# The boundary between two blocks of a decoder trunk: sample tokens join the norms of their token group, and the second group's sums stand ahead of the first group's second norm

## The chip, the core and the metric

The kernel runs on one core of one Trainium2 chip, in one launch. The metric is the device time of an execution in microseconds, the median of several runs. TensorE is PE in the profile (its weight loads PEld), VectorE is DVE, ScalarE is ACT, GpSimd is POOL, and SyncE is SP, whose queue issues most of the DMAs.

## What is computed

The reference is one step of a decoder trunk with two layers. Each layer has a token mixer (a gated DeltaNet in layer 0, an HGRN in layer 1) and then a feed-forward block with a short convolution. 1024 prompt tokens and 64 sample tokens (8 sequences of 8) share all weights; the width is 1024. What matters here is what stands between two blocks:

```python
for layer in range(DEPTH):
    sh1, sc1, g1, sh2, sc2, g2 = jnp.split(mod, N_MOD, axis=-1)
    h = _rmsnorm(x, norm_pre_mix[layer]) * (1 + sc1) + sh1
    out, S, ... = mixer(h, ...)
    x = x + (1 + g1) * _rmsnorm(out, norm_post_mix[layer])      # boundary: norm, gate, residual,
    h = _rmsnorm(x, norm_pre_ffn[layer]) * (1 + sc2) + sh2      # and the next block's norm
    out, fbuf = _conv_ffn(h, ...)
    x = x + (1 + g2) * _rmsnorm(out, norm_post_ffn[layer])
```

`_rmsnorm` divides a token's 1024 values by the root of their mean square. The scales, shifts and gates are one vector for the prompt and one for each sample sequence.

## The kernel before

Activations lie transposed: 1024 channels are 8 tiles of 128 partitions (the index m), and tokens run along the free axis. Tokens are cut into three groups. In the order in which every stage takes them they are called 0, 1 and 2 here, as in the strings below. Group 0 has 256 prompt tokens and the 64 sample tokens behind them (its matmuls are 320 wide), groups 1 and 2 have 384 prompt tokens each. Matmuls run on a high and a low part of every operand, so each step over 128 channels is three matmuls (L113 to L115). A block ends with an output product whose first half is done for all groups and whose second half (tile `pf`) is left to the boundary; the next block begins with products named `pg` (feed-forward) or `pp` (HGRN) on its input h.

`boundary()` (L330 to L400) is called four times: after the DeltaNet mixer, after the first feed-forward block, after the HGRN mixer, and at the end. It runs stages in the order of a string (L35 to L37): ORDM after a mixer, ORDF after the first feed-forward block, ORDL at the end. The stages of a group are:

- S (`st_sum`): per m the last twelve matmuls of the output (`pf`), their sum into `acc` on DVE (L352; L354 for the sample tokens), the squares on ACT (L236), their column sums on PE (`pn`, L228), a copy by ACT (`sqp`, L242) and a small product that leaves one sum per token and partition (`pc`, L245).
- R (`st_res`): 1/sqrt on DVE in some twelve tiny instructions (L251, L85 to L91), its spread over 128 partitions by PE (L218), and per m the gate (L364, DVE), the residual (L366, on POOL or DVE by the tables POOLM, POOLF and POOLL) and a DMA of the new residual to HBM.
- P (`st_pre`): the next block's norm, which squares the residual that R left (L236), sums it (L228, L242, L245), takes 1/sqrt, spreads it (L218), and makes h in three steps per m: L264 on DVE, L265 on ACT, L266 on DVE.
- s (`st_smp`): residual and next norm of the 64 sample tokens alone: squares (L280), a reduction of 1.0 us on DVE (L282), a product (L283), a 1/sqrt chain of their own (tiles `nwss`, `nwts`, `snr`), the spread (L275), and the elementwise steps (L380 to L382, L299 to L305), twice the whole way.

The program order of the stages is the order of priority of a scheduler that writes one fixed queue for each engine; an engine takes its queue in order. Buffers bound how far PE can run ahead: `pf`, `pg` and `pp` share a ring of three PSUM banks, and squares and `sqp` share a ring of two SBUF tiles, each of which holds two squares. A `pf` of tile m needs the bank that DVE's L352 of tile m-3 left.

Of the kernel before, what the change touches and what calls it, by code (L numbers as in the profile page):

```python
# [13 lines left out]
AF = mybir.ActivationFunctionType  # L14
ALU = mybir.AluOpType
# [3 lines left out]
D = 1024  # L19
# [23 lines left out]
def trunk_kernel(ctx: ExitStack, tc: tile.TileContext, a: dict, o: dict):  # L43
# [7 lines left out]
    def big(tag, shape=(128, NTOK), dt=F32, name=None, bufs=None):  # L51
        return main.tile(list(shape), dt, tag=tag, name=name or tag, bufs=bufs or {"xp": 2, "wraw": 3, "whl": 3}.get(tag, 1))
# [4 lines left out]
    def ps(tag, name=None):  # L57
        return psp.tile([128, 512], F32, tag=tag, name=name or tag, bufs={"mm": 3, "mx": 3, "rc": 2}[tag])
# [146 lines left out]
    def mod(l, i):  # L205
        return mods[l][:, 8 * i:8 * i + 8, :]
# [11 lines left out]
            mm(rb[:, 128 * j:128 * j + 128], r[:, j:j + 1].to_broadcast([128, 128]), ident, start=True, stop=True)  # L218
        return rb

    def row_sums(src, n):


        pn = ps("rc", name="pn")

        def add(m, s):
            q = m % 4
            return mm(pn[32 * q:32 * q + 32, :n], ones[:, :32], s, start=(m < 4), stop=(m >= 4), tile_position=(0, 32 * q))  # L228

# [12 lines left out]
        nc.scalar.activation(pb[:, :n], pn[:, :n], AF.Copy)  # L242
        pc = ps("mx", name="pc")
        for j in range(n // 128):
            mm(pc[:, 384 + j:385 + j], pb[:, 128 * j:128 * j + 128], selq, start=True, stop=True)  # L245
        return pc

    def row_rsqrt(pc, nt):

        v = small("pnv", [128, 3], bufs=2)  # L250
        nc.vector.tensor_scalar(v[:, :nt], pc[:, 384:384 + nt], 1.0 / D, EPS, op0=ALU.mult, op1=ALU.add)  # L251
        r = small("pnr", [128, 3], bufs=2)
        rsqrt(r[:, :nt], v[:, :nt], nt, "a")
        return bcast_rows(pc, r, nt)

    def prenorm(l, xg, n, isc, ish, hgt):

        rb = row_rsqrt(row_sums(xg, n), n // 128)
        sc, sh = mod(l, isc), mod(l, ish)
        pt = big("D10", [128, 2, 512], name="pnt")  # L260
        for m in range(8):
            t = pt[:, m % 2, :n]
            h = hgt[:, 0, m, :n]
            nc.vector.scalar_tensor_tensor(t, xg(m), sc[:, m, 0:1], rb[:, :n], op0=ALU.mult, op1=ALU.mult)  # L264
            nc.scalar.activation(h, t, AF.Identity, bias=sh[:, m, 0:1])  # L265
            nc.vector.scalar_tensor_tensor(hgt[:, 1, m, :n], t, sh[:, m, 0:1], h.bitcast(F32), op0=ALU.add, op1=ALU.subtract)  # L266
# [69 lines left out]
    def boundary(step, l, ig, kind, acc, acc_s, fin, nxt, hname):  # L336


        hgs = [None] * 3
        gw = mod(l, ig)  # L340
        pcs = [None] * 3

        def part(g):
            t0, n = GRP[g][0], GP[g]
            return t0, n, lambda m: acc[m][:, t0:t0 + n]

        def st_sum(g):
            t0, n, am = part(g)

            def total(m):  # L350
                p = fin(g, m)
                nc.vector.tensor_tensor(am(m), am(m), p[:, :n], op=ALU.add)  # L352
                if g == 2:
                    nc.vector.tensor_tensor(acc_s[:, m, :], acc_s[:, m, :], p[:, 256:320], op=ALU.add)  # L354
                return am(m)

            pcs[g] = row_sums(total, n)

        def st_res(g):
            t0, n, am = part(g)  # L360
            xg = load_x(step, g)
            rb = row_rsqrt(pcs[g], n // 128)
            for m in range(8):
                nc.vector.scalar_tensor_tensor(am(m), am(m), gw[:, m, 0:1], rb[:, :n], op0=ALU.mult, op1=ALU.mult)  # L364
                eng = nc.gpsimd if m in (POOLM if kind == 1 else POOLF if nxt is not None else POOLL)[GORD.index(g)] else nc.vector
                eng.tensor_tensor(am(m), am(m), xg(m), op=ALU.add)  # L366
                nc.sync.dma_start(out=xd[step + 1][m, :, t0:t0 + n], in_=am(m))

        def st_pre(g):
            t0, n, am = part(g)  # L370
            if nxt is not None:
                hgs[g] = new_hg(g, hname + str(g))
                prenorm(nxt[0], am, n, nxt[1], nxt[2], hgs[g])

        def st_smp():
            x_s = load_xs(step)
            pc = ps("mx", name="pcs")
            t = ssum(acc_s, pc, 0)
            rb = srow(pc, 0)
            nc.vector.tensor_tensor(v4(t), v4(acc_s), seqb(gw), op=ALU.mult)  # L380
            nc.vector.tensor_tensor(t, t, rb, op=ALU.mult)
            nc.vector.tensor_tensor(x_s, x_s, t, op=ALU.add)  # L382
            nc.gpsimd.dma_start(out=xsd[step + 1], in_=x_s)
            if nxt is not None:
                prenorm_s(nxt[0], nxt[1], nxt[2], hgs[2], x_s, pc)

        for w in (ORDM if kind == 1 else ORDF if nxt is not None else ORDL).split():
            if w == "s":
                st_smp()
            else:  # L390
                dict(S=st_sum, R=st_res, P=st_pre)[w[0]](GORD[int(w[1])])
# [1124 lines left out]
```

## Time and profile before

| what | value |
|---|---|
| median of three runs | 3280.22 us (3267.7 to 3284.62) |
| the profiled execution | 3271.93 us, its span 3270.2 us |
| PE busy | 3156.9 us, 97% |
| DVE, ACT, POOL busy | 1667.2, 1099.0, 275.9 us |
| the boundaries in the span | about 811 to 915, 1688 to 1790, 2371 to 2475 and 3205 to 3270 us |

PE is busy nearly all the time, so the profile is read for the stretches in which it is not. Rows of the timeline give the start of a group of equal instructions, its duration, engine, line, what it writes and reads, how many there are, and in brackets how long the engine was idle just ahead of it and what ended that. A table of windows gives each engine's busy time in a stretch and the granted TensorE clock (PEclk, 1.00 is 2.4 GHz and .50 is 1.2 GHz).

### The profile page before, as it was taken

Reading aid. Unit: us, or ns where it says so; the run is one execution under the profiler, and the core shown is the slowest. Engines: PE = TensorE matmul, PEld = TensorE weight load, DVE = VectorE, ACT = ScalarE, POOL = GpSimd, SP = SyncE. Lnnn points to the kernel's source line nnn. Section 1 sums busy time; section 2 is a strip of 40 time slices with the busy share of each in tenths; the row PEclk is TensorE's granted clock in tenths of the full one; section 3 lists DMA queues with packets and bytes.
Section 4 is the critical chain, followed back from the end, with each engine's and each line's share of the span. In section 5 each row is a group of like instructions: output and inputs, shape, how many; then the busy total and the mean of one; then the engine's idle time right before and its main releaser. Section 6 shows DMA issues by size and latency. Waiting matters only on the chain.

```text
span 3270.2 us, 61821 instructions
## 1 busy us (share of the span) xinstructions
PE 3156.9 (97%) x25457; PEld 2940.0 (90%) x25457; DVE 1667.2 (51%) x3819; ACT 1099.0 (34%) x2619; POOL 275.9 (8%) x623
## 2 busy tenths in 40 slices
PE   7999999999899999999998999999998999999997
PEld 5888888889799999999996999999888999999997
DVE  6776777773742333333357555554465233334345
ACT  5444444443433312222234333332343332222222
POOL 0111111110100000000000000000010000000002
PEclk9999999999999999999998999999999999999999
DMA  6333333234322222222322111122621111111113
GB/s 208 96 106 102 99 105 97 80 115 157 97 76 86 84 85 84 81 86 81 95 71 92 64 61 58 59 86 66 199 91 50 46 46 43 46 46 46 41 62 106
DMA packets 164642, 277.94 MB, mean 85 GB/s; under 512 B 20064, under 2 KB 91488, under 8 KB 164360
## 3 DMA queue, kind: packets, MB, share of 16 engines
q1 hardware_dynamic: 145976, 236.28, 22.3%
q0 software_dynamic: 14976, 37.08, 3.8%
q8 instruction: 200, 3.28, 0.4%
q10 hardware_dynamic: 3408, 0.63, 0.1%
q14 instruction: 82, 0.67, 0.1%
HBM read 222.44 MB, written 51.43 MB: 84 GB/s over the span
## 4 chain that ended last, share of the span: by engine, by line
PE 88%; DVE 5%; ACT 2%; DMA 2%; issue 2%; POOL 1%; ACTq 0%; SPq 0%; DVEq 0%; POOLq 0%
PE pp L114 7%; PE pp L113 7%; PE pp L115 6%; PE pu L113 5%; PE pg L113 5%; PE pg L114 5%; PE pg L115 5%; PE pu L115 5%; PE pu L114 5%; PE pd L113 5%; PE pd L115 5%; PE pd L114 5%; PE pf L113 1%; PE pf L114 1%; PE pf L115 1%
## 5 line engine op out<-in xcount | busy, mean ns | idle before, releaser
L113 PE MATMUL pp<-h,wi 128*128 128x384 f32 (+1 forms) x1536 | 516.2, 338 | 3.3 <-ACT h L304 2.5
L114 PE MATMUL pp<-h,wi 128*128 128x384 f32 (+1 forms) x1536 | 516.9, 337 | 0.7 <-DVE h L305 0.6
L115 PE MATMUL pp<-h,wi 128*128 128x384 f32 (+1 forms) x1536 | 514.6, 336 | 1.7 <-issue 1.7
L113 PE MATMUL pg<-h,wg 128*128 128x384 f32 (+1 forms) x1056 | 346.6, 329 | 0.0
L114 PE MATMUL pg<-h,wg 128*128 128x384 f32 (+1 forms) x1056 | 345.5, 328 | 0.8 <-DVE h L305 0.8
L113 PE MATMUL pu<-h,wu 128*128 128x384 f32 (+1 forms) x1056 | 346.3, 328 | 0.0
L115 PE MATMUL pg<-h,wg 128*128 128x384 f32 (+1 forms) x1056 | 346.0, 328 | 0.0
L115 PE MATMUL pu<-h,wu 128*128 128x384 f32 (+1 forms) x1056 | 344.8, 327 | 0.0
L114 PE MATMUL pu<-h,wu 128*128 128x384 f32 (+1 forms) x1056 | 344.3, 326 | 0.0
L113 PEld LDWEIGHTS pp<-h,wi 128*128 128x128 f32 x1536 | 291.5, 190 | 19.6 <-issue 11.3
L113 PE MATMUL pd<-mh,wd 128*128 128x384 f32 (+1 forms) x912 | 299.6, 330 | 0.0
L114 PEld LDWEIGHTS pp<-h,wi 128*128 128x128 f32 x1536 | 291.5, 190 | 7.0 <-DVE wi L107 1.2
L115 PE MATMUL pd<-mh,wd 128*128 128x384 f32 (+1 forms) x912 | 297.4, 326 | 0.0
L114 PE MATMUL pd<-ml,wd 128*128 128x384 f32 (+1 forms) x912 | 297.1, 326 | 0.0
L115 PEld LDWEIGHTS pp<-h,wi 128*128 128x128 f32 x1536 | 291.4, 190 | 5.6 <-issue 3.5
L113 PEld LDWEIGHTS pu<-h,wu 128*128 128x128 f32 x1056 | 198.2, 188 | 7.8 <-issue 6.2
L113 PEld LDWEIGHTS pg<-h,wg 128*128 128x128 f32 x1056 | 199.0, 189 | 6.2 <-issue 4.9
L114 PEld LDWEIGHTS pg<-h,wg 128*128 128x128 f32 x1056 | 199.0, 188 | 2.5 <-issue 1.2
L598 DVE TENSOR_TENSOR facc<-facc,pd 128x384 f32<-128x384 f32 (+1 forms) x192 | 97.5, 510 | 203.2 <-PE pd L115 203.2
L115 PEld LDWEIGHTS pg<-h,wg 128*128 128x128 f32 x1056 | 199.1, 189 | 0.0
L115 PEld LDWEIGHTS pu<-h,wu 128*128 128x128 f32 x1056 | 198.2, 188 | 0.0
L114 PEld LDWEIGHTS pu<-h,wu 128*128 128x128 f32 x1056 | 198.2, 188 | 0.0
(450 smaller groups left out, 5708.6 us busy)
## 6 DMA issues: line engine op xcount, KB each, us to landing
adaw<-in_ada_w SPq DMA_DIRECT2D x96, 512.0 KB, 3.9
wgr<-in_w_gu SPq DMA_DIRECT2D x88, 256.0 KB, 2.8
wur<-in_w_gu SPq DMA_DIRECT2D x88, 256.0 KB, 2.6
wir<-in_w_gin SPq DMA_DIRECT2D x64, 256.0 KB, 2.7
wdr<-in_w_dn SPq DMA_DIRECT2D x64, 256.0 KB, 2.5
wir<-in_w_hin SPq DMA_DIRECT2D x64, 256.0 KB, 2.7
og<-ohl SPq DMA_DIRECT2D x32, 384.0 KB, 8.2
xg<-xd SPq DMA_DIRECT2D x24, 384.0 KB, 4.7
```

The lines of the kernel that those rows point to most:

```text
L113: mm(out, wh, rh(k), start=(first and i == 0), stop=False)
L114: mm(out, wh, rl(k), start=False, stop=False)
L115: mm(out, wl, rh(k), start=False, stop=(last and i == len(ks) - 1))
L598: nc.vector.tensor_tensor(am, am, p[:, :n], op=ALU.add)
```

## The change

The stage s is gone. The squares of the sample tokens stand beside those of group 0, so that the `pn` matmuls of that group are 320 wide, one more `pc` matmul takes their sums, and a third column of the small tiles carries them through the group's 1/sqrt chain. One more spread (128x64) gives their factor. Their gate and residual are part of R of group 0, their norm is part of P of group 0. The orders are new, too: the sums S1 stand ahead of P0, and after a mixer S2 stands ahead of P1, as it did after the feed-forward block before.

```diff
-ORDM = "S0 R0 P0 S1 s R1 P1 S2 R2 P2"
-ORDF = "S0 R0 P0 S1 s R1 S2 P1 R2 P2"
-ORDL = "S0 S1 R0 s R1 S2 R2 P0 P1 P2"
+ORDM = "S0 R0 S1 P0 R1 S2 P1 R2 P2"
+ORDF = "S0 R0 S1 P0 R1 S2 P1 R2 P2"
+ORDL = "S0 S1 R0 R1 S2 R2"
...
-    def row_sums(src, n):
+    def row_sums(src, n, smp=None):
...
+        n0, n = n, n + (0 if smp is None else NS)
...
-                nc.scalar.activation(s, src(m), AF.Square)
+                nc.scalar.activation(s[:, :n0], src(m), AF.Square)
+                if smp is not None:
+                    nc.scalar.activation(s[:, n0:], smp[:, m, :], AF.Square)
...
+        if smp is not None:
+            mm(pc[:64, 386:387], pb[:, n0:n], selq, start=True, stop=True)
...
-        rsqrt(r[:, :nt], v[:, :nt], nt, "a")
+        if smp:
+            nc.vector.memset(v[64:, 2:3], 1.0)
+            nc.vector.tensor_scalar(v[:64, 2:3], pc[:64, 386:387], 1.0 / D, EPS, op0=ALU.mult, op1=ALU.add)
+            rsqrt(r, v, 3, "a")
+            mm(pc[:, 256:320], r[:64, 2:3].to_broadcast([64, 128]), ident[:64, :64], start=True, stop=True)
+        else:
+            rsqrt(r[:, :nt], v[:, :nt], nt, "a")
...
-    def prenorm(l, xg, n, isc, ish, hgt):
+    def prenorm(l, xg, n, isc, ish, hgt, x_s=None):
...
+        if x_s is not None:
+            norm_apply_s(l, isc, ish, hgt, x_s, small("S2", [128, 8, NS], name="sqs"), srow_b(rb), slice(0, 8))
...
+            if g == 2:
+                t = small("S2", [128, 8, NS], name="sqs")
+                nc.vector.tensor_tensor(v4(t), v4(acc_s), seqb(gw), op=ALU.mult)
+                nc.vector.tensor_tensor(t, t, srow_b(rb), op=ALU.mult)
+                nc.vector.tensor_tensor(smp[0], smp[0], t, op=ALU.add)
+                nc.gpsimd.dma_start(out=xsd[step + 1], in_=smp[0])
...
-        def st_smp():
...
-                prenorm_s(nxt[0], nxt[1], nxt[2], hgs[2], x_s, pc)
```

(In the code g is 2 for the group that the strings call 0.) The line numbers of the changed kernel differ: its L365 is L352 here, L379 is L364, L277 to L279 are L264 to L266, L237 and L239 are L236, L229 is L228, L245 is L242, L248 and L250 are L245, and L313 to L317 are L301 to L305.

The queues show where the work went. DVE's queue in the first boundary, around the last four sums of group 2 into `acc` (tiles acc_9356 to acc_9503 are m = 4 to 7). Before:

```order
L89 TENSOR_TENSOR nwts<-snr 64x1
L364 SCALAR_TENSOR_TENSOR acc_9454<-acc_9454,mod_91,pc 128x384
L90 TENSOR_TENSOR nwts<-nwts,nwxs 64x1
L364 SCALAR_TENSOR_TENSOR acc_9503<-acc_9503,mod_91,pc 128x384
L91 SCALAR_TENSOR_TENSOR snr<-nwts,snr 64x1
L352 TENSOR_TENSOR acc_9356<-acc_9356,pf 128x384
L89 TENSOR_TENSOR nwts<-snr 64x1
L352 TENSOR_TENSOR acc_9405<-acc_9405,pf 128x384
L90 TENSOR_TENSOR nwts<-nwts,nwxs 64x1
L352 TENSOR_TENSOR acc_9454<-acc_9454,pf 128x384
```

The same place after the change:

```order
L277 SCALAR_TENSOR_TENSOR pnt<-acc_9503,mod_91,pc 128x256
L379 SCALAR_TENSOR_TENSOR acc_9258<-acc_9258,mod_91,pc 128x384
L279 SCALAR_TENSOR_TENSOR h_9943<-pnt,mod_91,h_9943 128x256 x2
L379 SCALAR_TENSOR_TENSOR acc_9307<-acc_9307,mod_91,pc 128x384
L379 SCALAR_TENSOR_TENSOR acc_9356<-acc_9356,mod_91,pc 128x384
L379 SCALAR_TENSOR_TENSOR acc_9405<-acc_9405,mod_91,pc 128x384
L379 SCALAR_TENSOR_TENSOR acc_9454<-acc_9454,mod_91,pc 128x384
L379 SCALAR_TENSOR_TENSOR acc_9503<-acc_9503,mod_91,pc 128x384
L365 TENSOR_TENSOR acc_9356<-acc_9356,pf 128x384
L365 TENSOR_TENSOR acc_9405<-acc_9405,pf 128x384
L365 TENSOR_TENSOR acc_9454<-acc_9454,pf 128x384
L365 TENSOR_TENSOR acc_9503<-acc_9503,pf 128x384
```

The sixteen instructions of group 0's norm, and three of the sample tokens with them, now stand right ahead of these sums, in between those of R1; before, they stood among the sums of S1, and what stood between those of R1 was the sample tokens' 1/sqrt.

ACT's queue in the same boundary, with tile numbers. Before, where pn_10110 are the sums of P1 and sq_10184 the squares of S2:

```order
L236 ACTIVATE sq_10124<-acc6_9454 128x384
L236 ACTIVATE sq_10124<-acc7_9503 128x384
L242 ACTIVATE sqp_10131<-pn_10110 128x384
L236 ACTIVATE sq_10184<-acc0_9160 128x384
L236 ACTIVATE sq_10184<-acc1_9209 128x384
L236 ACTIVATE sq_10215<-acc2_9258 128x384
L236 ACTIVATE sq_10215<-acc3_9307 128x384
L304 ACTIVATE h12_9785<-sqs_10027 128x8x64
```

After, where pn_10086 are the sums of S2 and sq_10227 the squares of P1:

```order
L237 ACTIVATE sq_10118<-acc3_9307 128x384
L278 ACTIVATE h12_9943<-pnt_10008,mod0_91 128x256
L316 ACTIVATE h12_9943<-sqs_10002 128x8x64
L278 ACTIVATE h12_9943<-pnt_10008,mod0_91 128x256 x7
L237 ACTIVATE sq_10153<-acc4_9356 128x384
L237 ACTIVATE sq_10153<-acc5_9405 128x384
L237 ACTIVATE sq_10184<-acc6_9454 128x384
L237 ACTIVATE sq_10184<-acc7_9503 128x384
L245 ACTIVATE sqp_10219<-pn_10086 128x384
L237 ACTIVATE sq_10227<-acc0_9160 128x384
L237 ACTIVATE sq_10227<-acc1_9209 128x384
```

P1's eight squares moved from ahead of S2's to behind the last of them and its copy.

PE's queue in the same boundary, around the spread for P1 (L218). Before, three matmuls of it stand among the products `pg`, ahead of the last sums of S2:

```order
L113 MATMUL pg<-h_9785,wg 128x320
L114 MATMUL pg<-h_9785,wg 128x320
L115 MATMUL pg<-h_9785,wg 128x320
L113 MATMUL pg<-h_9785,wg 128x320
L218 MATMUL pc<-c_ident,pnr 128x128 x3
L228 MATMUL pn<-sq,ones 32x384 x4
L114 MATMUL pg<-h_9785,wg 128x320
```

After, the spreads for P1 and R2 are one row of six, right behind all of P1's sums:

```order
L113 MATMUL pg<-h_9943,wg 128x320
L114 MATMUL pg<-h_9943,wg 128x320
L115 MATMUL pg<-h_9943,wg 128x320
L229 MATMUL pn<-sq,ones 32x384 x8
L248 MATMUL pc<-c_selq,sqp 128x1 x3
L218 MATMUL pc<-c_ident,pnr 128x128 x6
L113 MATMUL pg<-h_10225,wg 128x384
```

The spread for P1 moved behind S2, and now goes together with that for R2.

## Rows read from the trace of the kernel before

**Rows 1.** The page's first part: busy time, share of the span, instructions.

```profile
PE 3156.9 (97%) x25457; PEld 2940.0 (90%) x25457; DVE 1667.2 (51%) x3819; ACT 1099.0 (34%) x2619; POOL 275.9 (8%) x623
```

**Rows 2.** What PE waited for: us in total, times, longest us.

```profile
PE pn L228 <- ACT sq L236: 28.7, 20, 4.7
...
PE pcs L275 <- DVE snr L91: 5.7, 1, 5.7
```

**Rows 3.** Windows of the first boundary: us; busy time by engine; PEclk, DMA share, GB/s.

```profile
880.00:898.00 18.00, 13.26 (x92) 12.03 (x96) 15.53 (x39) 7.07 (x13) 0.00 (x0) 1.00 0.10 35
898.00:908.30 10.30, 6.88 (x32) 4.62 (x25) 5.70 (x24) 5.10 (x13) 2.08 (x9) 0.50 0.27 96
```

**Rows 4.** Timeline of DVE in the first boundary: P0's norm, R1, last sums of S2.

```profile
846.44 0.55 DVE L352 TENSOR_TENSOR acc<-acc,pf 128x384 f32<-128x384 f32 x1
846.91 0.88 DVE L266 SCALAR_TENSOR_TENSOR h<-pnt,mod,h 128x256 fp32r<-128x256 f32 x2
847.70 0.87 DVE L264 SCALAR_TENSOR_TENSOR pnt<-acc,mod,pc 128x256 f32<-128x256 f32 x2
...
860.53 0.68 DVE L382 TENSOR_TENSOR x_s<-x_s,sqs 128x512 f32<-128x512 f32 x1
...
863.44 0.60 DVE L364 SCALAR_TENSOR_TENSOR acc<-acc,mod,pc 128x384 f32<-128x384 f32 x1
...
865.34 0.60 DVE L364 SCALAR_TENSOR_TENSOR acc<-acc,mod,pc 128x384 f32<-128x384 f32 x1
865.86 0.78 DVE L89 TENSOR_TENSOR nwts<-snr 64x1 f32<-64x1 f32 x1
...
871.38 0.54 DVE L352 TENSOR_TENSOR acc<-acc,pf 128x384 f32<-128x384 f32 x1
```

**Rows 5.** Timeline of PE in the first boundary: R1's spread, P1's, P2's sums.

```profile
862.23 0.83 PE L218 MATMUL pc<-c_ident,pnr 128*128 128x128 f32 x6
...
871.97 0.44 PE L113 MATMUL pf<-og,wo 128*128 128x384 f32 x1 [1.40 <-DVE acc L352]
...
879.83 0.93 PE L218 MATMUL pc<-c_ident,pnr 128*128 128x128 f32 x6
...
897.67 1.23 PE L228 MATMUL pn<-sq,ones 128*32 128x384 f32 x8 [4.74 <-ACT sq L236]
...
903.83 1.44 PE L245 MATMUL pc<-c_selq,sqp 128*128 128x1 f32 x6 [0.67 <-ACT sqp L242]
```

**Rows 6.** A window of the matmuls of `pf` (128x384) alone, in the first boundary.

```profile
829.10:832.20 3.10, 3.10 (x19) 3.10 (x19) 0.98 (x2) 1.00 0.00 0
```

**Rows 7.** Timeline of ACT in the first boundary: the last of P1's squares.

```profile
872.43 0.52 ACT L236 ACTIVATE sq<-acc 128x384 f32<-128x384 f32 x1 [0.44 <-POOL acc L366]
```

**Rows 8.** Timeline of PE in the second boundary, after the feed-forward block.

```profile
1733.51 0.83 PE L218 MATMUL pc<-c_ident,pnr 128*128 128x128 f32 x6
...
1747.11 0.63 PE L113 MATMUL pp<-h,wi 128*128 128x320 f32 x1 [2.51 <-ACT h L304]
1747.94 1.50 PE L228 MATMUL pn<-sq,ones 128*32 128x384 f32 x8 [0.20 <-ACT sq L236]
...
1763.24 2.93 PE L218 MATMUL pc<-c_ident,pnr 128*128 128x128 f32 x12 [2.44 <-DVE pnr L91]
...
1785.19 0.83 PE L245 MATMUL pc<-c_selq,sqp 128*128 128x1 f32 x6 [0.33 <-ACT sqp L242]
```

**Rows 9.** Timeline of DVE in the second boundary.

```profile
1746.31 1.01 DVE L352 TENSOR_TENSOR facc<-facc,pf 128x384 f32<-128x384 f32 x2
...
1766.74 1.90 DVE L266 SCALAR_TENSOR_TENSOR h<-pnt,mod,h 128x384 fp32r<-128x384 f32 x2
...
1770.14 1.14 DVE L266 SCALAR_TENSOR_TENSOR h<-pnt,mod,h 128x384 fp32r<-128x384 f32 x2
```

**Rows 10.** Timeline of ACT in the second boundary, between squares of P1 and `sqp`.

```profile
1757.81 1.28 ACT L1201 ACT_TABLE_LOAD   x1
```

**Rows 11.** Timeline of PE at the end: the last spread.

```profile
3258.54 1.65 PE L218 MATMUL pc<-c_ident,pnr 128*128 128x128 f32 x6 [2.42 <-DVE pnr L91]
```

More of the change, by code (lines that the diff above doesn't have):

```diff
@@ L245, in row_sums, with row_rsqrt @@
             mm(pc[:, 384 + j:385 + j], pb[:, 128 * j:128 * j + 128], selq, start=True, stop=True)
+        if smp is not None:
+            mm(pc[:64, 386:387], pb[:, n0:n], selq, start=True, stop=True)
         return pc
-    def row_rsqrt(pc, nt):
+    def row_rsqrt(pc, nt, smp=False):
         v = small("pnv", [128, 3], bufs=2)
@@ L252, in row_rsqrt @@
         r = small("pnr", [128, 3], bufs=2)
-        rsqrt(r[:, :nt], v[:, :nt], nt, "a")
+        if smp:
[5 more added lines that the diff above has]
+            rsqrt(r[:, :nt], v[:, :nt], nt, "a")
         return bcast_rows(pc, r, nt)
-    def prenorm(l, xg, n, isc, ish, hgt):
-        rb = row_rsqrt(row_sums(xg, n), n // 128)
+    def prenorm(l, xg, n, isc, ish, hgt, x_s=None):
+        rb = row_rsqrt(row_sums(xg, n, x_s), n // 128, x_s is not None)
         sc, sh = mod(l, isc), mod(l, ish)
+        if x_s is not None:
+            norm_apply_s(l, isc, ish, hgt, x_s, small("S2", [128, 8, NS], name="sqs"), srow_b(rb), slice(0, 8))
         pt = big("D10", [128, 2, 512], name="pnt")
@@ L291, in v4, with srow_b @@
         return t.rearrange("p m (s t) -> p m s t", t=8)
-    def prenorm_s(l, isc, ish, hgt, x_s, pc):
-        t = ssum(x_s, pc, 256)
-        norm_apply_s(l, isc, ish, hgt, x_s, t, srow(pc, 256), slice(0, 8))
+    def srow_b(pc):
+        return pc[:, 256:256 + NS].unsqueeze(1).to_broadcast([128, 8, NS])
     def norm_apply_s(l, isc, ish, hgt, x_s, t, rb, ms):
@@ L341, in boundary @@
         pcs = [None] * 3
+        smp = []
         def part(g):
@@ L355, in total @@
                 return am(m)
-            pcs[g] = row_sums(total, n)
+            pcs[g] = row_sums(total, n, acc_s if g == 2 else None)
         def st_res(g):
@@ L361, in st_res @@
             xg = load_x(step, g)
-            rb = row_rsqrt(pcs[g], n // 128)
+            if g == 2:
+                smp.append(load_xs(step))
+            rb = row_rsqrt(pcs[g], n // 128, g == 2)
             for m in range(8):
@@ L367, in st_res @@
                 nc.sync.dma_start(out=xd[step + 1][m, :, t0:t0 + n], in_=am(m))
+            if g == 2:
+                t = small("S2", [128, 8, NS], name="sqs")
[3 more added lines that the diff above has]
+                nc.gpsimd.dma_start(out=xsd[step + 1], in_=smp[0])
         def st_pre(g):
@@ L372, in st_pre @@
                 hgs[g] = new_hg(g, hname + str(g))
-                prenorm(nxt[0], am, n, nxt[1], nxt[2], hgs[g])
-        def st_smp():
[L376 to L384, printed above, removed]
-                prenorm_s(nxt[0], nxt[1], nxt[2], hgs[2], x_s, pc)
+                prenorm(nxt[0], am, n, nxt[1], nxt[2], hgs[g], smp[0] if g == 2 else None)
         for w in (ORDM if kind == 1 else ORDF if nxt is not None else ORDL).split():
[L388 to L391, printed above, removed]
+            dict(S=st_sum, R=st_res, P=st_pre)[w[0]](GORD[int(w[1])])
         return hgs
```

## The prediction

> **What bounds the kernel now.** The page's first part comes first: PE is busy 97% of the span [rows 1], so the time is PE's work plus the stretches in which PE stands still or runs at the lower clock. The change leaves nearly all matmuls alone, so only these stretches can move. What PE waited for tells where they are: the dearest single cause is the column sums waiting for ACT's squares, 28.7 us in twenty waits, which is the work of the boundaries; the sample tokens' own 1/sqrt costs 5.7 us once [rows 2]. The windows of the first boundary show both kinds of loss: from 880 to 898 us PE is busy 13.26 of 18.00 us, and from 898.0 to 908.3 it is busy 6.88 of 10.30 us at a granted clock of .50 (1.2 GHz), after having been half idle just before [rows 3]. So I follow PE, DVE and ACT through one boundary, from R1's spread to P2's sums. P2's sums are my mark: behind them ACT frees the banks of the waiting products in both queues, and what is left of PE's work is the same. The shift of that mark is what a boundary costs or gains. A boundary after a mixer occurs twice (about 811 and 2371 us, the same queues), the one after the feed-forward block once, the end once.
>
> **The change part by part.** *Sample tokens.* Taken away per boundary are two reductions, two chains of 1/sqrt on 64 rows, two squares of 512 columns and two spreads; added are eight squares of 64 columns, twice, one column in an existing chain, one `pc` and one spread. DVE saves most of it, but little of it stands where PE waits, except in the second boundary: there PE waits 5.71 us for that 1/sqrt [rows 2] and then 2.51 us for the sample tokens' h [rows 8]. Both named waits must go. What is late there next is counted below.
>
> *P0 behind S1.* This is the edit that I think decides. Before, P0's norm lies under the sums of S1: two L264 and two L266 take 0.79 and 0.78 us, and one sum L352 of 0.47 us goes with them, from 846.44 to 848.48 [rows 4]; PE has S1's matmuls meanwhile, so it costs nothing. After, DVE's queue has these sixteen instructions between R1's spread and the last four sums of S2. This cover is gone, and what waits behind them is S2: tile m = 7 of `pf` needs the bank of m = 4, which the first of these sums frees. Before, that sum starts at 871.38 and the matmul that waited for it at 871.97 [rows 4, 5].
>
> *Term 1, from R1's spread to that sum.* Before: 862.23 [rows 5] to 871.38, 9.15 us. After: 1.2 us from spread to first use (862.23 to 863.44 [rows 4, 5]), four pairs of P0 at 1.57 us (the two figures above), 6.3 us, three instructions of the sample tokens at 0.60 to 0.68 us (the size of L382 [rows 4]), 2.0 us, and R1's eight L364 at 0.52 us (865.34 to 865.86 [rows 4]), 4.2 us: 13.7 us. P0's L266 now also lie beside POOL's residual adds. Beside such an add two L266 took 1.90 us, without one 1.14 [rows 9], so 0.76 us; I take one such pair, 14.5 us. That is 5.4 us more. The spread itself comes earlier, since L381 and L382 and the sample tokens' tiny instructions leave the chain ahead of it: two at 0.60 us and some 0.2 us, 1.4 us. Term 1: +4.0 us; ends +1.5 (the spread 3 us earlier, no add met) and +6 (two more pairs meet an add).
>
> That a VectorE instruction is held up by an add on GpSimd is also what the Trainium skill says, in "SBUF — State Buffer", section "Who interferes with whom": with two SBUF inputs it contends with a GpSimd instruction that reads SBUF, and whichever starts second is blocked for the whole of the other. The row shows part of an add, not a whole one. By the rule all four pairs could be held, and term 1 would end some 2 us higher; that speaks against the change, which puts P0 where R1's adds are.
>
> *Term 2, from that sum to P1's spread.* Before: 871.38 to 879.83 [rows 4, 5], 8.45 us, because P1's squares ran as R1's residuals came, the last at 872.43 [rows 7], ahead of S2's. After, they stand behind all of S2's squares and their copy. First come twelve matmuls of m = 7 (19 of them in 3.10 us [rows 6], so 2.0 us), a sum of 0.54 us [rows 4] and a square of 0.52 us [rows 7]: 3.1 us. For the rest the second boundary is the pattern, since there S2 stood ahead of P1 already and the two spreads were one row: from the last sums of S2 at 1747.94 to that row at 1763.24, 15.3 us [rows 8]. Of these 1.28 us are a table load between P1's squares and their copy [rows 10], which the first boundary has not: 14.0 us. Together 17.1 us, 8.6 us more; as part of the pattern ran at 1.2 GHz, which I don't expect to the same extent, I take 7.5. Ends +5.5 and +10.5.
>
> *Term 3, from P1's spread to P2's sums.* Before: 879.83 to 903.83 [rows 5], 24.0 us, with R2's scaling behind P1's norm and a wait of 4.74 us in P2's sums. After, P1's norm and R2's scaling share DVE from one row of spreads on, as in the second boundary: 1763.24 to 1785.19 [rows 8], 21.95 us. Term 3: -2 us; ends -4 and 0.
>
> First boundary: 4.0 + 7.5 - 2 = +9.5 us; twice, +19. If all ends fell one way it would be 3 or 16.5; I take 5 to 13 us each.
>
> *Second boundary.* S2 was ahead of P1 before, so terms 2 and 3 are 0. P0's norm, which lay under S1's matmuls here too, joins R1's stretch, which already held the sample tokens. Two of the last sums ran at 1746.31 [rows 9]. After: from R1's spread at 1733.51 [rows 8], the same 13.7 us and five residual adds that DVE keeps by POOLF (0.47 us each, the size of L352), 16.0 us, less 1 us for an earlier spread: 1748.5. With one pair beside an add, 1749.3. So +3 us; the wait for the sample tokens' h (1747.11) is hidden behind it. One more us if a bank is late as above: +4, ends +1 and +7. The 5.71 and 2.51 us don't come back as gain, because what stands in their place is as late.
>
> *The end.* No P there; S0, S1, R0, R1, S2, R2 stay as they were, without the sample stage, and the last spread at 3258.54 [rows 11] hangs on S2. 0 us, ends -2 and +1.5.
>
> Sum: 19 + 4 + 0 = +23 us; from the ends so taken +9 (10 + 1 - 2) to +34 (26 + 7 + 1.5). On the profiled execution, 3271.93 us, that is 3295; this execution is 8.3 us under the median, 3280.22, on which it is 3303. The new time is a median too, so I go nearer to that: 3301 us.
>
> **The rivals.** *Even.* DVE gets rid of some 7 us of sample work per boundary (two reductions of 1.0 us, two chains, squares on ACT), and if the queue's head start is worth that, the late norm is paid for: term 1 falls to its lower end, term 2 to 4 us because PE stays at full speed, and a boundary after a mixer costs 3 us, the second one gains 4 to 6. For: the waits in rows 2. Against: the saved work is not on the stretch from R1's spread on, save for the tiny instructions between the L364. Time: 3280 +- 8 us.
>
> *Faster.* PE stays fed: group 0's h is complete before S2's last tile needs a bank, so that PE takes `pg` products under S2's late sums, and all named waits go: 5.71 + 2.51 in the second boundary, 4.74 + 0.67 in each after a mixer, and half of 10.30 us at half clock in each. That is 8.2 + 10.8, and up to 5 more: some 20 us less, 3260 us. It decides if DVE is through P0 before PE has run `pf` to m = 7. Against: PE's queue has m = 7 ahead of the `pg` products, and an engine takes its queue in order.
>
> *Worse than forecast.* The idle stretch of PE, ahead of the late sum, is followed by a stretch at 1.2 GHz, as at 898.0 [rows 3], and the pairs of P0 all meet POOL's adds: the upper ends, +33 us, 3313 us.
>
> *The change doesn't do what it says.* P0 in front of S2's sums would be harmless if the queue had the sums first; the queues show otherwise, so this has no chance of its own.
>
> **How the numbers follow.** Forecast 0.50, even 0.28, faster 0.14, worse 0.08. 0.5% is about what a measurement can tell from no change, 16 us here: 3264 to 3297. The forecast's own range is 3291 to 3311; about two thirds of it lie over 3297. Slower: 0.34 + 0.08, and 0.02 of the even case: 0.44. Same: 0.16 + 0.26: 0.42. Faster: 0.14. The range leaves out the faster case and half of the worse one: 3270 to 3314.
>
> **What would show it.** In DVE's timeline, the first of S2's last four sums about 14 us behind R1's spread, and PE idle for some 8 us just ahead of it; a stretch at .50 there. P1's spread at about 891 us and as a row of twelve. P2's sums some 9 us later against the first `pf` of the boundary. The second boundary without waits on `snr`, but with one of similar size on `acc` sums or P0's h. If PE's idle time ahead of S2's last tile is under 3 us, term 1 is wrong; if P1's spread follows the late sum by under 12 us, term 2 is; if the second boundary got shorter by over 5 us, the named waits were what bound it.

## The result, and the profile after

| | before | after |
|---|---|---|
| median of six runs each | 3276.03 us (3267.7 to 3284.62) | 3300.05 us (3297.24 to 3306.24) |
| ratio after to before | | 1.0077, interval 1.0064 to 1.009 |
| the profiled execution, its span | 3271.93, 3270.2 us | 3299.28, 3297.5 us |

The change makes the kernel 24 us slower, 0.77%; 3301 us was forecast. In the page's first part PE has the same 25457 matmuls, as in [rows 1], and 11.6 us more busy time (the mean granted clock of the two traces is 0.986 before and 0.980 after); DVE has 84 instructions and 19.5 us less:

```profile
PE 3168.5 (96%) x25457; PEld 2946.6 (89%) x25457; DVE 1647.7 (50%) x3735; ACT 1102.7 (33%) x2668; POOL 278.3 (8%) x623
```

So work was saved, and time was lost. Where, PE's waits in the whole span say (us in total, times, longest us). The wait for the sample tokens' 1/sqrt of [rows 2] is gone; what PE waits for instead are sums into the accumulators, 9.2 us at a time after a mixer and 11.6 us after the feed-forward block:

```profile
PE pn L229 <- ACT sq L237: 21.0, 13, 2.5
PE pf L113 <- DVE acc L365: 18.4, 2, 9.2
PE pp L113 <- DVE facc L365: 11.6, 1, 11.6
PE pc L218 <- DVE pnr L91: 10.0, 5, 2.4
```

The first boundary in PE's timeline of the changed kernel; these lines answer to [rows 5]. PE runs out of `pf` after R1's spread, and 16 us pass until the tile that needs the late sum:

```profile
855.77 1.38 PE L218 MATMUL pc<-c_ident,pnr 128*128 128x128 f32 x10
...
871.65 0.69 PE L113 MATMUL pf<-og,wo 128*128 128x384 f32 x1 [9.20 <-DVE acc L365]
...
888.85 2.93 PE L218 MATMUL pc<-c_ident,pnr 128*128 128x128 f32 x12 [2.44 <-DVE pnr L91]
...
910.05 1.44 PE L248 MATMUL pc<-c_selq,sqp 128*128 128x1 f32 x6 [0.67 <-ACT sqp L245]
```

DVE's timeline of the same stretch answers to [rows 4]. P0's L279 and R1's L379 stand ahead of S2's last sums L365, and DVE is busy from 856.51, its first use of the spreads, to 872.5. The last line is the sum of m = 7, whose matmuls waited for the first of these sums:

```profile
861.21 1.63 DVE L279 SCALAR_TENSOR_TENSOR h<-pnt,mod,h 128x256 fp32r<-128x256 f32 x2
...
864.07 1.61 DVE L279 SCALAR_TENSOR_TENSOR h<-pnt,mod,h 128x256 fp32r<-128x256 f32 x2
...
866.90 1.60 DVE L279 SCALAR_TENSOR_TENSOR h<-pnt,mod,h 128x256 fp32r<-128x256 f32 x2
...
868.43 2.70 DVE L379 SCALAR_TENSOR_TENSOR acc<-acc,mod,pc 128x384 f32<-128x384 f32 x5
871.05 1.47 DVE L365 TENSOR_TENSOR acc<-acc,pf 128x384 f32<-128x384 f32 x3
875.85 0.55 DVE L365 TENSOR_TENSOR acc<-acc,pf 128x384 f32<-128x384 f32 x1 [3.33 <-PE pf L115]
```

Windows of it (us; busy time of PE, PEld, DVE, ACT, POOL; PEclk, DMA share, GB/s) answer to [rows 3]. From 854.6 to 867.5 PE is busy 7.85 of 12.90 us, and behind that the granted clock is .50 (1.2 GHz) for 7.5 us, in which PE stands still for more than half:

```profile
854.60:867.50 12.90, 7.85 (x46) 6.06 (x45) 11.33 (x26) 4.26 (x9) 2.88 (x4) 0.92 0.23 67
867.50:875.00 7.50, 3.35 (x10) 3.35 (x11) 5.02 (x9) 1.45 (x3) 5.56 (x6) 0.50 0.51 186
```

To compare traces whose stretches ahead of a boundary differ, every boundary is measured from its first `pf` matmul. A second trace of the kernel before was taken among the experiments; its execution (3275.45 us) lies nearer to the median. Lengths to the last `pc` matmul of P2, the mark of the prediction, and from one first `pf` to the next (the last column to the end of the span):

| | 1st | 2nd | 3rd | first pf to next first pf |
|---|---|---|---|---|
| before | 93.7 | 97.8 | 93.7 | 876.8, 683.0, 834.4, 64.8 |
| before, second trace | 95.9 | 98.2 | 96.2 | 879.5, 684.3, 837.0, 64.9 |
| after | 106.7 | 106.0 | 107.0 | 890.8, 689.2, 848.8, 64.3 |

Against the second trace the boundaries with what follows them take 11.3, 4.9 and 11.8 us more, the end 0.6 less: 27.4 us. The same code ahead of the first boundary was 3.6 us shorter, so that the spans differ by 23.8 us; the medians differ by 24.0. Against the first trace, which the prediction was worked out from, the same sum is 34.1 us (14.0, 6.2, 14.4 and -0.5): one program's traces differ by so much.

### The profile page after: what moved, and what is told of

The parts are those of the page before. It is cut to its first block, busy times and chain, and to the rows that moved or that the text cites. A ratio compares the mean times of both kernels' runs of the same rounds, so it can differ in the third digit from the quotient of the medians.

```text
span 3297.5 us, 61790 instructions
## 1 busy us (share of the span) xinstructions
PE 3168.5 (96%) x25457; PEld 2946.6 (89%) x25457; DVE 1647.7 (50%) x3735; ACT 1102.7 (33%) x2668; POOL 278.3 (8%) x623
## 4 chain that ended last, share of the span: by engine, by line
PE 87%; DVE 7%; ACT 2%; DMA 2%; issue 2%; ACTq 0%; SPq 0%; POOL 0%; DVEq 0%; POOLq 0%
PE pp L114 6%; PE pp L113 6%; PE pp L115 6%; PE pu L113 5%; PE pu L115 5%; PE pu L114 5%; PE pg L113 5%; PE pg L115 5%; PE pg L114 5%; PE pd L113 5%; PE pd L115 5%; PE pd L114 5%; PE pf L115 2%; PE pf L113 2%; PE pf L114 2%
## 5 line engine op out<-in xcount | busy, mean ns | idle before, releaser
L113 PE MATMUL pp<-h,wi 128*128 128x384 f32 (+1 forms) x1536 | 515.7, 337 | 12.6 <-DVE facc L365 11.6
```

What stands on the lines that cost most here:

```text
L113: mm(out, wh, rh(k), start=(first and i == 0), stop=False)
```

## The experiments

All kernels are one of the two with other order strings, unless told otherwise. "Joined" means that sample tokens are part of group 0, as after the change. Lengths are those of the table above.

### The join alone, and the orders alone

The changed kernel with the orders of before:

```diff
-ORDM = "S0 R0 S1 P0 R1 S2 P1 R2 P2"
-ORDF = "S0 R0 S1 P0 R1 S2 P1 R2 P2"
+ORDM = "S0 R0 P0 S1 R1 P1 S2 R2 P2"
+ORDF = "S0 R0 P0 S1 R1 S2 P1 R2 P2"
```

> Sample tokens joined as in the changed kernel, but the three orders as before without the sample stage (P0 ahead of S1 again, P1 ahead of S2 after a mixer, S2 ahead of P1 after the feed-forward block as before). From the first pf to P2's sums the boundaries take 93.7, 97.8 and 93.7 us before and 106.7, 106.0 and 107.0 us after. Theory 'orders' (the time is lost because P0's norm stands ahead of S2's last sums, and P1's squares behind S2's): about 92, 93 and 92 us, since the sample tokens' own chains are gone and nothing is late; ratio to before 0.996 to 0.999. Theory 'join' (the wider group-0 path, sixteen more ACT squares and three more DVE steps in P0 cost it): about 105 us each, ratio 1.006 to 1.009.

Measured: ratio 1.0015 (1.0003 to 1.0027); 100.9, 96.3 and 100.8 us. Both theories miss: the join gains nothing, it costs some 5 us. Its profiled execution lay far over the median, so it was traced a second time:

> The kernel of the run with the join alone, for a second trace: its profiled execution (3288.94 us) was the slowest of ten, 9.5 us over their median, so one trace may not stand for it. If the boundaries after a mixer are 100.9 and 100.8 us again, the join costs 7 us there in every execution, and the difference lies elsewhere; if they are 94 to 97 us, the first trace was a disturbed one, and the join is worth nothing either way.

Measured: 98.6, 98.6 and 98.5 us, 3281.39 us. Neither figure: the lengths move by 2.3 us from one execution to the next. (From first `pf` to first `pf` it is 882.5 and 839.8 us behind a mixer, 3 us over the second trace of before.) So the kernel before was traced again, too:

> The kernel before, unchanged, for a second trace: how far do the lengths of the boundaries and of the stretches between them repeat? Boundaries of 93.7, 97.8 and 93.7 us within 1 us would carry the comparisons of 2 us and more made so far; the stretch ahead of the first boundary (811.2 us before, 804.4 us after the change, the same code) should vary by several us if it is chance.

Measured: 95.9, 98.2 and 96.2 us, and 808.0 us ahead of the first boundary. The boundaries don't repeat within 1 us. From here on differences of lengths under 2.5 us carry nothing, and ratios of medians decide. (Where the 2.2 us come from is told at the end.)

The other half, the new orders with the sample tokens in their own stage:

```diff
-ORDM = "S0 R0 P0 S1 s R1 P1 S2 R2 P2"
-ORDF = "S0 R0 P0 S1 s R1 S2 P1 R2 P2"
-ORDL = "S0 S1 R0 s R1 S2 R2 P0 P1 P2"
+ORDM = "S0 R0 S1 P0 s R1 S2 P1 R2 P2"
+ORDF = "S0 R0 S1 P0 s R1 S2 P1 R2 P2"
+ORDL = "S0 S1 R0 s R1 S2 R2"
```

> Sample tokens in a stage of their own as before, but S1 ahead of P0, and S2 ahead of P1, everywhere; the sample stage right behind P0. Theory 'orders': P0's sixteen instructions and the sample tokens' chains both stand ahead of S2's last sums, so the boundaries take at least what they take after the change, 105 to 112 us after a mixer and 105 to 110 after the feed-forward block; ratio 1.008 to 1.013. Theory 'join': 94, 98 and 94 us as before, ratio 1.000 within 0.002.

Measured: ratio 1.0061 (1.0039 to 1.0083); 104.0, 95.4 and 105.0 us. The orders make most of the loss, in the boundaries after a mixer; ratio and lengths lie between the two theories, nearer to the first. They don't lose it in the changed kernel's way, though: here P0 and the sample tokens stand ahead of R1's 1/sqrt as well, R1's spread comes 58.3 us behind the first `pf` (after the change 51.4), and a `pf` waits 3.46 us for a sum, not 9.20:

```profile
868.70 0.69 PE L113 MATMUL pf<-og,wo 128*128 128x384 f32 x1 [3.46 <-DVE acc L352]
869.19 1.48 PE L218 MATMUL pc<-c_ident,pnr 128*128 128x128 f32 x6
```

The second boundary did not get longer, against the expectation, and DVE's timeline of that kernel shows what is different there: P0's norm ends at 1751, then come S2's last sums, and only then R1's scaling L364. The first of these sums starts 52.6 us behind the boundary's first `pf` (1698.8), where the changed kernel has 64.9:

```profile
1750.32 0.86 DVE L266 SCALAR_TENSOR_TENSOR h<-pnt,mod,h 128x256 fp32r<-128x256 f32 x2
1751.37 0.53 DVE L352 TENSOR_TENSOR facc<-facc,pf 128x384 f32<-128x384 f32 x1
...
1753.79 0.61 DVE L364 SCALAR_TENSOR_TENSOR facc<-facc,mod,pc 128x384 f32<-128x384 f32 x1
```

The same string gave a late sum or none, since a scheduler turns it into queues. The sum's place in the queue is what goes with the loss there, not the string.

### The two edits of the order apart

P0 ahead of S1 everywhere, S2 and P1 as after the change behind a mixer and swapped in the second boundary:

```diff
-ORDM = "S0 R0 S1 P0 R1 S2 P1 R2 P2"
-ORDF = "S0 R0 S1 P0 R1 S2 P1 R2 P2"
+ORDM = "S0 R0 P0 S1 R1 S2 P1 R2 P2"
+ORDF = "S0 R0 P0 S1 R1 P1 S2 R2 P2"
```

> Joined; P0 ahead of S1 in all boundaries; S2 ahead of P1 after a mixer, P1 ahead of S2 after the feed-forward block. It sets the two edits of the order apart. By the prediction's terms as the two traces give them (term 1 +6.5, term 2 +9.4, term 3 -2.8 in the first boundary) a boundary after a mixer keeps terms 2 and 3 and loses term 1: about 100 us; the second boundary takes the order that a mixer's boundary had, and goes to about 92 us. Rival: S2 ahead of P1 costs only because the sums are already late, then 94 us after a mixer. Ratio by the terms about 1.002, by the rival 0.997.

Measured: ratio 0.9994 (0.9982 to 1.0007); 96.4, 93.6 and 97.1 us. The loss is gone, with S2 still ahead of P1 after a mixer; ratio and lengths lie between what the terms gave (1.002, about 100 us) and the rival (0.997, 94 us). In this kernel's DVE timeline only R1's eight L379 stand between its spread (866.47) and S2's last sums, of which two are left there:

```profile
867.34 4.29 DVE L379 SCALAR_TENSOR_TENSOR acc<-acc,mod,pc 128x384 f32<-128x384 f32 x8 [0.46 <-PE pc L218]
871.55 0.55 DVE L365 TENSOR_TENSOR acc<-acc,pf 128x384 f32<-128x384 f32 x1
```

The other way round, P0 behind S1 but P1 ahead of S2:

```diff
-ORDM = "S0 R0 S1 P0 R1 S2 P1 R2 P2"
-ORDF = "S0 R0 S1 P0 R1 S2 P1 R2 P2"
+ORDM = "S0 R0 S1 P0 R1 P1 S2 R2 P2"
+ORDF = "S0 R0 S1 P0 R1 P1 S2 R2 P2"
```

> Joined; S1 ahead of P0 in all boundaries; P1 ahead of S2 in all. By the terms a boundary after a mixer keeps term 1 (P0's norm ahead of S2's last sums, PE without work for 7 to 9 us) and loses terms 2 and 3: about 98 to 100 us; the second boundary about 99 (its late sum stays, the row of twelve spreads goes). Rival: the late sum is cheap when P1's squares need not wait for S2's: 94 us. Ratio by the terms about 1.004, by the rival 0.998.

Measured: ratio 1.0038 (1.0021 to 1.0055); 101.8, 96.3 and 102.0 us. The ratio is that of the terms; the lengths lie 2 us over what they gave after a mixer and 3 under in the second boundary. What PE waits for is another thing, though. The sum of m = 4 slipped in ahead of P0 (858.55), three sums remain behind, no `pf` lacks a bank, and PE waits 7.48 us for ACT's squares instead. Of this kernel, DVE's and then PE's timeline:

```profile
858.55 0.54 DVE L365 TENSOR_TENSOR acc<-acc,pf 128x384 f32<-128x384 f32 x1
...
874.27 1.47 DVE L365 TENSOR_TENSOR acc<-acc,pf 128x384 f32<-128x384 f32 x3
```

```profile
859.69 0.83 PE L218 MATMUL pc<-c_ident,pnr 128*128 128x128 f32 x6
...
873.93 1.51 PE L229 MATMUL pn<-sq,ones 128*32 128x384 f32 x8 [7.48 <-ACT sq L237]
...
882.56 0.93 PE L218 MATMUL pc<-c_ident,pnr 128*128 128x128 f32 x6
```

From R1's spread to the late sums 14.6 us pass here as well. So it is the stretch on DVE that costs, by whichever wait PE notices it. That a further bank would not have helped the changed kernel follows only by analogy; no kernel with one was run. The last line is P1's spread: it comes 8.3 us behind the late sums, as before the change (8.45 and 10.8 in its two traces), where the changed kernel has 17.8.

The last corner, the kernel before (sample tokens separate, P0 ahead of S1) with S2 and P1 swapped:

```diff
-ORDM = "S0 R0 P0 S1 s R1 P1 S2 R2 P2"
-ORDF = "S0 R0 P0 S1 s R1 S2 P1 R2 P2"
+ORDM = "S0 R0 P0 S1 s R1 S2 P1 R2 P2"
+ORDF = "S0 R0 P0 S1 s R1 P1 S2 R2 P2"
```

> The kernel before (sample tokens separate, P0 ahead of S1) with one swap: S2 ahead of P1 after a mixer, P1 ahead of S2 after the feed-forward block. With the runs so far it fills the table of three edits: joined or not, P0 ahead of S1 or behind, S2 ahead of P1 or behind. Theory 'interaction' (S2 ahead of P1 costs 3 us on its own, about 10 only where P0 stands behind S1): a boundary after a mixer 95 to 97 us against 93.7, the second boundary 95 to 97 against 97.8. Rival 'S2 ahead of P1 costs the 9.4 - 2.8 us that term 2 and term 3 came to, wherever P0 stands': 100 us after a mixer. Ratio by the first 1.001, by the rival 1.004.

Measured: ratio 1.001 (1.0001 to 1.002); 98.7, 91.5 and 101.5 us. The ratio is that of the first theory, but only because the second boundary fell further than expected; the lengths after a mixer lie over its 95 to 97 us, one of them over the rival's 100. By them S2 ahead of P1 costs about 3 to 5 us after a mixer (against 95.9 and 96.2) and P1 ahead of S2 gains 6 in the second boundary, of which the stretch behind it gives some back (681.4 us to the next first `pf`, against 684.3).

### What P0 costs where it stands

P0 behind S2, so that nothing of it is ahead of S2's sums:

```diff
-ORDM = "S0 R0 S1 P0 R1 S2 P1 R2 P2"
-ORDF = "S0 R0 S1 P0 R1 S2 P1 R2 P2"
+ORDM = "S0 R0 S1 R1 S2 P0 P1 R2 P2"
+ORDF = "S0 R0 S1 R1 S2 P0 P1 R2 P2"
```

> Joined; P0 behind S2 in all boundaries (S0 R0 S1 R1 S2 P0 P1 R2 P2), so that nothing but R1 stands ahead of S2's last sums. Theory 'P0's norm ahead of S2's sums is term 1': the time from R1's spread to the first of the late sums falls from 15.3 to about 5.3 us (1.2 plus eight L379), and no pf waits for a sum over 1.5 us. What it costs: h of group 0 comes after PE has run out of pf, so PE idles some 6 to 9 us there instead. Length of a boundary after a mixer 98 to 104 us. Rival: the late sum comes from something else (the sums wait for R1's residual adds, or for the chain): the stretch stays above 10 us.

Measured: one execution, 3305.2 us; 106.9, 102.4 and 106.2 us. From R1's spread (854.79) to the first late sum (859.97 in DVE's timeline) it is 5.2 us now, and no `pf` waits for it. That settles term 1's cause. With P0 out of the way R1's spread, too, comes 43.0 us behind the first `pf` (811.8), 8 us earlier than after the change. DVE's, then PE's timeline:

```profile
855.76 4.29 DVE L379 SCALAR_TENSOR_TENSOR acc<-acc,mod,pc 128x384 f32<-128x384 f32 x8 [1.03 <-PE pc L218]
859.97 1.47 DVE L365 TENSOR_TENSOR acc<-acc,pf 128x384 f32<-128x384 f32 x3
```

```profile
854.79 0.93 PE L218 MATMUL pc<-c_ident,pnr 128*128 128x128 f32 x6
...
867.78 0.34 PE L115 MATMUL pf<-og,wo 128*128 128x384 f32 x1
...
889.49 0.64 PE L113 MATMUL pg<-h,wg 128*128 128x320 f32 x1
```

But the boundary is as long as after the change, over the upper end expected: the products for group 0 now wait for P0, and from the last `pf` to the first `pg` 21.7 us pass. Of the three places tried, P0's norm is cheap only under the matmuls of S1.

R1's residual adds on DVE in place of POOL, the changed kernel else:

```diff
-POOLM = (range(8), range(8), ())
+POOLM = (range(8), (), ())
```

> The changed kernel, but after a mixer R1's eight residual adds run on DVE and not on POOL. After the change two L279 of P0 beside such an add took 1.60 to 1.63 us, without one 0.88. Theory 'the add on POOL holds them': without adds on POOL every pair takes 0.88 us, 2.2 us less over three pairs; DVE has eight adds of 0.47 us more, so that from R1's spread to S2's last sums the stretch grows from 15.3 to about 16.9 us, a boundary by 1 to 2 us. Rival: the pairs are slow for what they read and write (fp32r outputs beside ACT's h), then 1.6 us stays and the stretch is about 19 us.

Measured: one execution, 3304.27 us; 108.2, 101.6 and 108.3 us. The pairs of L279 take 0.88 us, and the stretch from R1's spread (859.94) to the first late sum is 16.8 us, both as the theory had it:

```profile
865.39 0.88 DVE L279 SCALAR_TENSOR_TENSOR h<-pnt,mod,h 128x256 fp32r<-128x256 f32 x2
...
876.75 1.48 DVE L365 TENSOR_TENSOR acc<-acc,pf 128x384 f32<-128x384 f32 x3
```

### A version that beats both

With P0 back under S1, what ends last runs from S2's sums over R2 to P2's. R2's scaling shares DVE with P1's norm there, as after the change. (In the kernel before it comes behind that norm: R2's sums are there at 882.75, its spread at 892.04, and DVE has P1's norm in between.) So R2 goes ahead of P1 after a mixer (changed kernel, joined):

```diff
-ORDM = "S0 R0 S1 P0 R1 S2 P1 R2 P2"
-ORDF = "S0 R0 S1 P0 R1 S2 P1 R2 P2"
+ORDM = "S0 R0 P0 S1 R1 S2 R2 P1 P2"
+ORDF = "S0 R0 P0 S1 R1 P1 S2 R2 P2"
```

> Joined, P0 ahead of S1, and after a mixer R2 ahead of P1 as well (S2 R2 P1 P2); the second boundary with P1 ahead of S2 as in the run with 96.4, 93.6 and 97.1 us. If the way from S2's sums over R2 to P2's sums is what ends last, R2's scaling no longer shares DVE with P1's norm (1.05 us for two L379 in every 2.6 us there) and the boundaries after a mixer fall to 91 to 94 us; ratio 0.996. Rival: PE then lacks h of group 1 and group 0's products run out sooner, the gain is given back, 96 to 98 us; ratio 1.000.

Measured: 3264.43 us, ratio 0.997 (0.9957 to 0.9982). This is the lowest median of the study, 11 us under the kernel before and 36 under the changed one. The lengths to P2's sums (81.4, 92.9 and 81.3 us) can't be compared after a mixer, because P1 now stands behind them; from first `pf` to first `pf` it is 876.5, 683.3 and 834.2 us, 3.0, 1.0 and 2.8 less than in the second trace of before, but within 0.3 us of the first (876.8, 683.0, 834.4); the profiled execution, 3272.29 us, is the second slowest of ten. So the ratio carries the gain, and the lengths don't place it. In its DVE timeline R2 has DVE to itself, two m in 1.99 us, where in the kernel with 96.4 us the first two L379 of R2 start 5.2 us apart (888.49 and 893.71), with P1's norm between them:

```profile
881.04 1.14 DVE L379 SCALAR_TENSOR_TENSOR acc<-acc,mod,pc 128x384 f32<-128x384 f32 x2 [1.03 <-PE pc L218]
882.10 1.02 DVE L381 TENSOR_TENSOR acc<-acc,xg 128x384 f32<-128x384 f32 x2
883.03 1.13 DVE L379 SCALAR_TENSOR_TENSOR acc<-acc,mod,pc 128x384 f32<-128x384 f32 x2
```

The same order in the second boundary, too:

```diff
-ORDF = "S0 R0 P0 S1 R1 P1 S2 R2 P2"
+ORDF = "S0 R0 P0 S1 R1 S2 R2 P1 P2"
```

> Joined, P0 ahead of S1, and R2 ahead of P1 in all three inner boundaries (S0 R0 P0 S1 R1 S2 R2 P1 P2). With that order after a mixer alone the kernel measured 0.997 of the kernel before. If the way over R2 to P2's sums bounds the second boundary as well, its time from the first pf to the first pf of the next boundary falls from 683.3 by 2 to 4 us and the ratio to 0.995 to 0.997. Rival: there P1's norm is wanted first, since the products of group 0 are fewer before ACT takes them; then 685 us or more and a ratio of 0.998 to 0.999.

Measured: ratio 0.9978 (0.9968 to 0.9988), 683.9 us there. Nothing gained that could be told; the intervals of the two overlap, and the length lies between the theory's and its rival's.

And with the sample tokens separate, as before:

```diff
-ORDM = "S0 R0 P0 S1 s R1 P1 S2 R2 P2"
-ORDF = "S0 R0 P0 S1 s R1 S2 P1 R2 P2"
+ORDM = "S0 R0 P0 S1 s R1 S2 R2 P1 P2"
+ORDF = "S0 R0 P0 S1 s R1 P1 S2 R2 P2"
```

> Sample tokens separate as before, R2 ahead of P1 after a mixer, P1 ahead of S2 after the feed-forward block (where the separate kernel with that order took 91.5 us against 97.8). It parts the join from the order in the version that beat the kernel before. If the gain comes from R2's place and the join is worth nothing, the ratio is 0.996 to 0.998, as with the join (0.997). If the join is needed for it, since the sample tokens' chains stand in R1's stretch, the ratio is 0.999 to 1.002.

Measured: ratio 0.9984 (0.9973 to 0.9995). About half of the gain on the kernel before comes without the join, and whether the join adds the rest is inside the intervals. What R2's place alone is worth shows against the kernels that differ in nothing else: joined from 0.9994 to 0.997, separate from 1.001 to 0.9984. That is 0.0024 and 0.0026, some 8 us, with the join or without.

## Why the prediction was right, point by point

The direction, the place and the size were right: 3301 us forecast, 3300.05 measured. That they lie within 1 us is luck: 3301 was taken between 3295 and 3303 us, and from the median of six runs, 3276.03, the same 23 us would have given 3299. The terms of a boundary after a mixer, by times behind its first `pf`. Before is the second trace (first `pf` at 808.0; spread 858.99, sum 868.14, P1's spread 878.95, P2's sums 902.84), after starts at 804.4:

| | before | after | moved by | term: forecast | measured |
|---|---|---|---|---|---|
| R1's spread | 51.0 | 51.4 | 0.4 | | |
| first late sum | 60.1 | 66.7 | 6.5 | term 1: +4.0 (1.5 to 6) | +6.5 |
| P1's spread | 71.0 | 84.5 | 13.5 | term 2: +7.5 (5.5 to 10.5) | +7.0 |
| P2's sums | 94.8 | 105.7 | 10.8 | term 3: -2 (-4 to 0) | -2.7 |

Against the first trace, the prediction's own (first `pf` at 811.2), the terms are +6.5, +9.4 and -2.8, and P2's sums come 13.0 us later, at the upper end of the 5 to 13 us that were forecast.

**Term 1** had the right cause: taking P0 out of the way brought the stretch to 5.2 us, moving it under S1 took the loss away. Its size was under the measured one for two reasons. The stretch itself is 15.3 us where 14.5 was summed: three of the four pairs of L279 met an add on POOL and not one, 1.63, 1.61 and 1.60 us against 0.88 without adds, which is 2.2 us and not 0.76; the first use of the spread and the sample tokens' instructions came 0.7 us cheaper. And the spread of R1 was to come 1.4 us earlier, which it did not. The step that failed there is "the spread itself comes earlier": it counted what leaves DVE's chain ahead of the spread, but the spread now goes in one row with P0's (x10 in PE's timeline), and that row waits for P0's sums. R1's own sums were there 7 us earlier; in PE's timeline of the changed kernel they are the first of these lines, P0's the second:

```profile
843.11 0.75 PE L248 MATMUL pc<-c_selq,sqp 128*128 128x1 f32 x6
...
850.15 0.50 PE L248 MATMUL pc<-c_selq,sqp 128*128 128x1 f32 x4
```

With P0 behind S2, R1's spread came at 43.0 us in place of 51.4, which bears this out. An order with R1's 1/sqrt alone ahead of P0's was not run.

On the price of the adds the Trainium skill had more than the one pair that the sum took ("SBUF — State Buffer", section "Who interferes with whom": a VectorE instruction with two SBUF inputs contends with a GpSimd instruction that reads SBUF, on ports that only one of the two holds at a time, so that the order of issue decides who is blocked). In both boundaries after a mixer three of P0's four pairs stood beside an add and were held, by 0.72 to 0.75 us, and the one without an add was not, so the trace agrees with the rule on who is held; the amount is the measured one. In the second boundary one instruction of P0 beside an add was held by only 0.2 us. In POOL's timeline the first of these adds starts 0.17 us behind the start of its pair (861.21):

```profile
861.38 1.18 POOL L381 TENSOR_TENSOR acc<-acc,xg 128x384 f32<-128x384 f32 x1 [2.87 <-DVE acc L379]
```

**Term 2** had the size, and its reason, P1's squares behind S2's, holds as far as P1's spread: from the first late sum to that spread it takes 8.3 us with P0 behind S1 and P1 ahead of S2, and 17.8 after the change; with P0 ahead of S1 it takes 9.7 in both traces of the join alone, and 14.0 (871.55 to 885.52) with S2 ahead of P1. The changed kernel has the late tile of m = 7 on top, whose sum comes 4.8 us behind the first late sum (875.85). What the prediction lacks is that this delay is no fixed price at the mark. With the tokens joined and P0 ahead of S1 it was made up behind the spread (21.2 us from P1's spread to P2's sums, against 29.5 and 27.2 in the join alone), and the ratio was 0.9994 against 1.0015. With P0 behind S1 it was not, 1.0077 against 1.0038; with the tokens separate it cost 3 to 5 us by the lengths. The kernels compared differ in the second boundary as well, so the split is not exact, and why it is made up in one case and not in the other is not settled.

**Term 3** was right within 1 us, by the pattern of the second boundary.

**The second boundary** was forecast at +4 us and came to +7.8 at the mark, +4.9 with what follows, which gives 3 us back. The wait for the sample tokens' 1/sqrt and that for their h went, as forecast, and 11.55 us for a sum came in their place. PE's timeline of the changed kernel, which answers to [rows 8]:

```profile
1744.14 1.38 PE L218 MATMUL pc<-c_ident,pnr 128*128 128x128 f32 x10
...
1760.75 0.60 PE L113 MATMUL pp<-h,wi 128*128 128x320 f32 x1 [11.55 <-DVE facc L365]
...
1778.90 2.93 PE L218 MATMUL pc<-c_ident,pnr 128*128 128x128 f32 x12 [2.44 <-DVE pnr L91]
...
1800.65 0.83 PE L248 MATMUL pc<-c_selq,sqp 128*128 128x1 f32 x6 [0.33 <-ACT sqp L245]
```

The stretch from R1's spread to the late sum (1760.06 in DVE's timeline) is 15.9 us, where 16.8 was summed (16.0 and one pair beside an add). Mis-sized was the spread again: 1 us earlier in the forecast, 3.3 us later in the trace (48.9 us behind the first `pf` against 45.6).

**The end** was forecast at 0 and shortened by 0.6 us; the ranges held for all but term 1 and, at the mark, the second boundary. Together the boundaries came to 27.4 us where 23 were summed, by the first trace to 34.1; the profiled times fit better than that, as the code ahead of the first boundary, which is the same, ran 3.6 us shorter in this execution.

Some figures of the working don't come out, without changing the forecast. Two more pairs beside an add would make term 1 +5.5 and not +6. PE was not half idle over the window ahead of 898.0 (13.26 of 18.00 us busy), only in its last part, which has the 4.74 us wait. The terms of the faster case add up to 24 us and not to 20.

**The rivals.** "Faster" fell by its own condition: DVE was not through P0 before PE needed the bank. "Even" fell too: DVE lost 19.5 us of work over the kernel (some 5 per boundary and not 7), and the join alone, which saves that work, gained no time. "Worse" had both its signs, the stretch at .50 and three of four pairs beside adds, but not its time. The join alone was taken to be free; it measured 1.0015, some 5 us, as part of after's 24. Why is not settled. In both kernels that join the tokens and keep P0 ahead of S1, R1's spread comes about 4 us later than before (55.1 to 55.5 us behind the first `pf`, against 51.0). But in the join alone that is made up by P1's spread (70.3 in both traces, against 71.0), and the time goes between there and R2's spread: 17.7 and 15.4 us, against 12.1 in the second trace of before. Nothing was run to test why.

## What to carry to other kernels

An instruction moved on a busy engine is priced by what stands behind it there: follow the queue to the next instruction that another engine waits for, and ask which work covers the place that it left and the place that it goes to. Work saved on an engine that is half idle bought nothing here: what counts is whether it stands between two waits of the engine that bounds. Where a scheduler makes the queues, two edits of a priority order need not add up, as they did not here; look at the queue that comes out, and measure the corners.

## What the hardware showed that was not expected

The same kernel, the same queue and the same waits gave two granted clocks. Windows of PE in the first boundary of the kernel before (us; PE busy; PEclk, DMA share, GB/s), first the trace of [rows 3], then the second one, both from 60 to 70 us behind the first `pf`. In both PE waits 1.40 us for the same sum just ahead:

```profile
871.20:876.20 5.00, 3.98 (x26) 1.00 0.93 262
876.20:881.20 5.00, 4.61 (x36) 1.00 0.42 156
```

```profile
868.00:873.00 5.00, 4.01 (x20) 0.78 0.96 272
873.00:878.00 5.00, 5.00 (x22) 0.54 0.46 163
```

In the first the clock stays at 1.00 (2.4 GHz), in the second it falls to its lower level (1.2 GHz) for most of that time (.78 and .54 in the mean), and P1's spread comes 71.0 us behind the first `pf` in place of 68.6. That is 2.2 us of the boundary's length, in a program that did not change; what decides between the two was not tried. By the two traces each of this kernel and of the join alone, a boundary's length from a single trace is good to some 2.5 us, no better.
